# Score products over all 128 rows, and the memory's keys and values from split operands, in the second block of a two-block network

## The chip, the cores and the metric

The kernel runs on one core of a Trainium2 chip. The metric is the device time of one execution in microseconds (us), as the median of the runs. The core has five engines with a queue of their own each: TensorE (PE, with weight loads shown apart as PEld), VectorE (DVE), ScalarE (ACT), GpSimd (POOL) and SyncE (SP), which issues most of the transfers (DMA).

## The reference, cut to what matters

Two blocks of two layers each run over 512 tokens of width 1024. The change lies in the second block's token mixing: in the branch in which every query attends to selected keys (8 heads of 64), and in the branch that attends to a memory of 256 tokens (4 heads of 128).

```python
def dsa_branch(q, k, v, iq, ik, iw, positions):
    q = rotary(q.reshape(B, S, ATT_HEADS, ATT_HEAD_DIM), positions)
    k = rotary(k.reshape(B, S, ATT_HEADS, ATT_HEAD_DIM), positions)
    ...
    _, sel = lax.top_k(score, n_sel)                     # by the index heads
    s = jnp.einsum('bqhd,bqkhd->bqhk', qb, kg) * (ATT_HEAD_DIM ** -0.5)
    p = jax.nn.softmax(jnp.where(valid, s, -jnp.inf), axis=-1)
    return jnp.einsum('bqhk,bqkhd->bqhd', p, vg)

def memory_branch(mq, mem, w_mem_kv):
    kv = jnp.einsum('bmd,de->bme', mem, w_mem_kv)        # [256, 1024] @ [1024, 1024]
    mk, mv = jnp.split(kv, 2, axis=-1)
    s = jnp.einsum('bshd,bmhd->bhsm', q, mk) * (MEM_HEAD_DIM ** -0.5)
    return jnp.einsum('bhsm,bmhd->bshd', jax.nn.softmax(s, axis=-1), mv)
```

## The kernel before

Everything is computed in float32. A large product is made of three products of reduced operands: `split` (L368) writes a tensor as a high part (a cast on ACT, L370) and a low part (a subtraction on DVE, L371), and `mm3` (L361) multiplies high by high, high by low and low by high into one bank of PSUM. Weights come as units of 128 x 1024 (512 KB) through `Stream` (L1946): `next` loads a unit into one of 3 raw tiles and splits it into one of 4 pairs of the ring; `raw` (L1958) hands out the unit as it is. Large activations take one of 11 tiles of the pool `g8`.

`mixing_` (L1226) is one layer's token mixing in the second block. It first calls `memory_kv` (L1416), which makes the keys and values of the memory for the layer. There both operands are plain float32, not split: one float32 product is two passes on PE (two weight loads and two matmuls in the trace). `flush` then turns the last normalised tokens of the part before, and the projections follow: index keys and queries, then, merged, the index (which keys are selected), the memory's attention and other projections; then, merged again, `heads` (rotary queries and keys of two heads at a time), `attention` (L1504) and the gates.

For each pair of heads `heads` makes q of 2 planes and k of 3 planes of 512 tokens. A plane of q holds one head: its high part in 64 rows (partitions), its low part in the other 64. A plane of k holds that head's high part twice, in both halves, and the third plane the low parts of both heads, one in each half. A score tile is thus the product over 128 rows (high and low of q by high of k, L1515) plus a product over the 64 rows of q's high part and k's low part (L1516). There are 32 score tiles in a layer: 4 pairs of heads, 4 query tiles of 128 tokens and 2 heads, with 128, 256, 384 or 512 keys. The scores are followed by the softmax on DVE and ACT, the turn of the probabilities (L1528) and the product with the values (L1541).

The order of the instructions on each engine, and when a tile of a pool is taken, come from the framework's scheduler, which goes by priority in program order and by its own estimate of times; the kernel fixes the order only by how it merges the chains.

Of the kernel before, what the change touches and what calls it, by code (L numbers as in the profile page):

```python
# [11 lines left out]
F32 = mybir.dt.float32  # L12
# [24 lines left out]
# ---------------------------------------------------------------- host layout  # L37


def fm_unit(w, cols):  # L40
    """Columns `cols` of w [K, N] (-1: zeros) as a stationary unit [128, K/128 * len(cols)]."""
    k = w.shape[0] // 128
    cols = np.asarray(cols)
    out = np.zeros((128, k, len(cols)), w.dtype)
    on = cols >= 0
    out[:, :, on] = w.reshape(k, 128, -1)[:, :, cols[on]].transpose(1, 0, 2)
    return out.reshape(128, -1)


def tok_units(w, c, kp):  # L50
    """Rows of two k tiles and 512 columns of w as a moving unit [128, 2 * 512]."""
# [8 lines left out]
def cols(v):  # L60
    """[n * 128] -> [128, n]"""
# [7 lines left out]
def layout(i):  # L69
# [66 lines left out]
    # second block  # L136
# [58 lines left out]
def shape_constants():  # L195
# [14 lines left out]
    # frequency, phase (of a cosine), sign  # L210
# [19 lines left out]
# ---------------------------------------------------------------- the kernel  # L230


def merge(*chains):
    """Runs generators side by side; each (generator, share) yields what a step weighs, or None when it
    waits for another. The one that is furthest behind goes next."""
# [13 lines left out]
def pipeline(n, *stages):  # L249
    """Stage s of item i beside stage s + 1 of item i - 1."""  # L250
# [8 lines left out]
class Lane:  # L259
    """Tiles of one chain of work: its own slots, so that chains do not wait for each other's."""  # L260
# [27 lines left out]
class Net:  # L288
# [20 lines left out]
    def part(self, name):  # L309
        """Room on chip for a part of the work."""  # L310
# [6 lines left out]
    def phase(self, name):  # L317
        """The same with banks of PSUM."""
# [3 lines left out]
    # ---- small helpers  # L322
# [9 lines left out]
    def room(self, dt):  # L332
        """Small tiles in one of the raw ones, until it is full."""
# [15 lines left out]
    def new_h(self):  # L349
        """Token-major tiles [4][128, 1024]."""  # L350
# [3 lines left out]
    def row(self, L, name, n):  # L354
        """A row of DRAM on every partition."""
# [5 lines left out]
    def mm3(self, ps, a, b, start, stop):  # L361
        """ps (+)= a.T @ b for operands (high, low)."""
# [5 lines left out]
    def split(self, hi, lo, src, engine=None):  # L368
        """hi + lo = src, in parts that the PE carries exactly."""
# [3 lines left out]
    def rsqrt(self, L, v, n, scale=1.0, add=EPS):  # L373
        """(v * scale + add) ** -0.5 of [128, n] (more than 0)."""
# [26 lines left out]
    # ---- layer norm of token-major tiles into token-major h and feature-major (high, low)  # L401
# [10 lines left out]
    def ln_norm(self, L, t, gb, spill=None, light=()):  # L412
        """The layer norm of h[t], in place."""
# [3 lines left out]
    def ln_stats(self, L, src):  # L417
        """Of rows in two halves: what normalises them."""
# [11 lines left out]
    def ln_apply(self, L, t, gb, spill, stats, after=None, light=()):  # L430
        """The normalised rows into h[t]; `after`: what GpSimd does first; `light`: the tiles with both halves past
        the vector engine's longer forms."""
# [29 lines left out]
    def flush(self, L):  # L462
        """The turns that the part before has left, so that the PE does not wait for them."""
# [17 lines left out]
    # ---- products with the streamed weights  # L481
    def fm(self, L, u, x):
        """One tile of 128 output features, all tokens: PSUM [128, 512]."""
# [5 lines left out]
    def fm_first(self, lanes, us, x, L):  # L489
        """The first units of a part, one to a bank of each lane: the first half of the tokens, what is left of  # L490
        their turns, and the other half."""
# [11 lines left out]
    def tokmaj(self, L, st, x, use):  # L503
        """use(t, PSUM [128, 512]): token-major, one token tile after the other, over 8 k tiles."""
# [10 lines left out]
    def tokpart(self, L, st, lhs, kt, first):  # L515
        """h (token-major) += the product over kt k tiles, the tokens innermost."""
# [12 lines left out]
    def tokfinal(self, L, st, lhs, kt, first, done, turn=None):  # L529
        """As tokpart, one token tile after the other, each handed to done(t) and, two tiles later, to turn(t)."""  # L530
# [20 lines left out]
    # ---- statistics over features that lie on partitions  # L551
    def feat_r(self, L, sq, n):
        """(mean of the squares + eps) ** -0.5 of the tokens of each tile: [128, 4]."""
# [7 lines left out]
    def feat_rsqrt(self, L, sq, n):  # L561
        """Rows (mean of the squares + eps) ** -0.5 of all tokens on every partition: PSUM [128, 512]."""
# [1442 lines left out]
```

## Time and profile before

| | |
|---|---|
| median of 3 runs | 3082.91 us (3081.3 to 3084.93) |
| span of the profiled execution | 3080.9 us |
| PE, DVE, ACT, POOL busy | 96%, 70%, 46%, 15% of the span |
| memory stage of the first and the second layer | from about 1370 to 1402 us, from about 2214 to 2252 us |
| attention stage of the first and the second layer | from about 1572 to 1800 us, from about 2422 to 2650 us |

The profile is of one execution, whose first and last instruction lie 3080.9 us apart; the runs' median is 2.0 us above that. A line of an engine in the timeline gives start, duration, engine, line of the program, operation, the tile it writes and those it reads, the shape and how many were merged. Products on PE overlap: the cost of one is the distance to the next start, not its duration. "issue" stands for time in which an engine waited for nothing that the profile shows.

### The profile page before, as it was taken

Reading aid. Unit: us, or ns where it says so; the run is one execution under the profiler, and the core shown is the slowest. Engines: PE = TensorE matmul, PEld = TensorE weight load, DVE = VectorE, ACT = ScalarE, POOL = GpSimd, SP = SyncE. Lnnn points to the kernel's source line nnn. Section 1 sums busy time; section 2 is a strip of 40 time slices with the busy share of each in tenths; the row PEclk is TensorE's granted clock in tenths of the full one; section 3 lists DMA queues with packets and bytes.
Section 4 is the critical chain, followed back from the end, with each engine's and each line's share of the span. In section 5 each row is a group of like instructions: output and inputs, shape, how many; then the busy total and the mean of one; then the engine's idle time right before and its main releaser. Section 6 shows DMA issues by size and latency. Waiting matters only on the chain. (4 is left out here: it accounts for less than half of the span.)

```text
span 3080.9 us, 38491 instructions
## 1 busy us (share of the span) xinstructions
PE 2959.6 (96%) x14258; PEld 2306.5 (75%) x14258; DVE 2155.6 (70%) x3441; ACT 1432.6 (46%) x2230; POOL 463.6 (15%) x427
## 2 busy tenths in 40 slices
PE   7999999999999999999999997999899999979996
PEld 6777888888777888887777786777577777867774
DVE  6884756565976755666875447999758754479997
ACT  4443433334344433324534433888445344238884
POOL 4311100004211000011101103110311011031103
PEclk9999999998999999999999998999899999989998
DMA  5121233333120332335232256999441322569993
GB/s 185 50 74 42 84 96 96 99 115 104 49 76 28 104 97 97 101 130 158 59 94 75 82 205 222 366 385 384 163 143 57 93 78 83 198 221 358 384 382 123
DMA packets 128512, 457.25 MB, mean 148 GB/s; under 512 B 15744, under 2 KB 16832, under 8 KB 126912
## 3 DMA queue, kind: packets, MB, share of 16 engines
q1 hardware_dynamic: 117696, 425.37, 40.0%
q0 software_dynamic: 7168, 16.79, 1.7%
q10 hardware_dynamic: 3456, 12.58, 1.1%
q8 instruction: 114, 1.87, 0.2%
q14 instruction: 78, 0.64, 0.1%
HBM read 428.99 MB, written 27.26 MB: 148 GB/s over the span
## 5 line engine op out<-in xcount | busy, mean ns | idle before, releaser
L364 PE MATMUL AP<-g,hi 128*128 128x512 f32 (+1 forms) x1824 | 712.7, 391 | 6.1 <-DVE g L1321 2.6
L365 PE MATMUL AP<-g,hi 128*128 128x512 f32 (+1 forms) x1824 | 703.0, 386 | 3.7 <-DVE g L371 3.7
L366 PE MATMUL AP<-g,lo 128*128 128x512 f32 (+1 forms) x1824 | 703.9, 386 | 0.0
L371 DVE TENSOR_TENSOR lo<-raw,hi 128x1024 fp32r<-128x1024 f32 x306 | 393.5, 1287 | 373.2 <-ACT hi L370 364.1
L370 ACT CAST hi<-raw 128x1024 fp32r<-128x1024 f32 x318 | 333.5, 1050 | 607.0 <-PE AP L365 406.7
L364 PEld LDWEIGHTS AP<-g,hi 128*128 128x128 f32 x1824 | 346.9, 190 | 81.8 <-issue 8.2
L365 PEld LDWEIGHTS AP<-g,hi 128*128 128x128 f32 x1824 | 347.2, 190 | 71.5 <-issue 4.3
L366 PEld LDWEIGHTS AP<-g,lo 128*128 128x128 f32 x1824 | 346.9, 190 | 68.8 <-issue 2.6
L371 DVE TENSOR_TENSOR lo<-g,hi 128x1024 fp32r<-128x1024 f32 x204 | 239.1, 1218 | 23.7 <-ACT hi L370 23.2
L370 ACT CAST hi<-g 128x1024 fp32r<-128x1024 f32 x204 | 207.0, 1050 | 50.5 <-PE AP L366 32.7
L371 DVE TENSOR_TENSOR lo<-wide,hi 128x1024 fp32r<-128x1024 f32 x180 | 211.0, 1217 | 23.9 <-ACT hi L370 23.4
L365 PE MATMUL HP<-lo,Txt 128*96 128x512 f32 x512 | 203.7, 398 | 0.0
L366 PE MATMUL HP<-hi,Txt 128*96 128x512 f32 x512 | 203.5, 397 | 0.0
L364 PE MATMUL HP<-hi,Txt 128*96 128x512 f32 x512 | 201.5, 400 | 1.1 <-ACT Txt L370 1.1
L370 ACT CAST hi<-wide 128x1024 fp32r<-128x1024 f32 x180 | 182.7, 1050 | 22.3 <-PE HP L366 18.3
L364 PE MATMUL AP<-hi,g 128*128 128x512 f32 x384 | 159.6, 419 | 2.7 <-DVE g L880 2.7
L366 PE MATMUL AP<-hi,g 128*128 128x512 f32 x384 | 152.9, 400 | 0.0
L365 PE MATMUL AP<-lo,g 128*128 128x512 f32 x384 | 152.3, 398 | 0.0
L364 PE MATMUL BP<-hi,g 128*128 128x512 f32 x352 | 136.8, 390 | 0.0
L365 PE MATMUL BP<-lo,g 128*128 128x512 f32 x352 | 136.6, 389 | 0.0
L366 PE MATMUL BP<-hi,g 128*128 128x512 f32 x352 | 134.0, 389 | 0.0
L1203 POOL TENSOR_TENSOR Bw<-Bw,Bw 128x512 f32<-128x512 f32 x26 | 43.7, 1681 | 459.0 <-DVE Bw L1202 384.0
(497 smaller groups left out, 5235.3 us busy)
## 6 DMA issues: line engine op xcount, KB each, us to landing
wide<-in_wmoeu SPq DMA_DIRECT2D x64, 1024.0 KB, 8.5
g<-in_wmoeu SPq DMA_DIRECT2D x64, 1024.0 KB, 8.1
raw<-in_wup SPq DMA_DIRECT2D x88, 512.0 KB, 3.5
g<-in_wmoed SPq DMA_DIRECT2D x34, 1024.0 KB, 8.6
wide<-in_wmoed SPq DMA_DIRECT2D x30, 1024.0 KB, 8.2
raw<-in_xwin SPq DMA_DIRECT2D x50, 512.0 KB, 3.7
raw<-in_xgate SPq DMA_DIRECT2D x48, 512.0 KB, 3.6
raw<-in_wdown SPq DMA_DIRECT2D x44, 512.0 KB, 3.5
```

The costliest lines, as they stand in the source:

```text
L364: mm(ps, a[0], b[0], start=start, stop=False)
L365: mm(ps, a[0], b[1], start=False, stop=False)
L366: mm(ps, a[1], b[0], start=False, stop=stop)
L370: self.nc.scalar.copy(hi, src)
L371: (engine or self.nc.vector).tensor_tensor(out=lo, in0=src, in1=hi.bitcast(F32), op=OP.subtract)
L1203: nc.gpsimd.tensor_tensor(out=u, in0=u, in1=sw, op=OP.add)
```

## The change

Three edits, all in the second block. k gets a fourth plane, so that the low part of each head has a plane of its own, with zeros in the other 64 rows (written by POOL); the second score product then runs over 128 rows, like the first. `memory_kv` splits the memory (4 pieces of two k tiles) and its weights into high and low and uses `mm3` in place of the float32 products; the two parts of the memory take two more tiles of `g8` while it runs. The pool weights `pw` and the value bias `bv` are allocated and loaded in the part `xmem`, after the index queries, in place of the start of `mixing_`. Comments and docstrings are removed too.

```diff
@@ mixing_
-        pw = kept("pw")
-        nc.sync.dma_start(pw, self.A[f"poolw{l}"])
-        bv = kept("bv")
-        src = self.A[f"bv{l}"]
-        nc.sync.dma_start(bv, bass.AP(tensor=src.tensor, offset=src.offset, ap=[[0, 128], [1, 512]]))
...
         with self.part(f"xmem{l}"):
+            pw, bv = kept("pw"), kept("bv")
+            nc.sync.dma_start(pw, self.A[f"poolw{l}"])
+            src = self.A[f"bv{l}"]
+            nc.sync.dma_start(bv, bass.AP(tensor=src.tensor, offset=src.offset, ap=[[0, 128], [1, 512]]))
...
-                q, k = (self.pp.tile([128, n, S], FR, tag="qk%d" % n, bufs=1, name=self.nm("qk")) for n in (2, 3))
+                q, k = (self.pp.tile([128, n, S], FR, tag="qk%d" % n, bufs=1, name=self.nm("qk")) for n in (2, 4))
...
                     ac.copy(k[at, i], rot[at])
-                    ve.tensor_tensor(out=k[at, 2], in0=rot[at], in1=k[at, i].bitcast(F32), op=OP.subtract)
+                    ve.tensor_tensor(out=k[at, 2 + i], in0=rot[at], in1=k[at, i].bitcast(F32), op=OP.subtract)
+                    nc.gpsimd.memset(k[to, 2 + i].bitcast(F32), 0.0)
                     ac.copy(k[to, i], rot[at])
@@ memory_kv
+        mem = [self.g8(FR, (128, 8, 256)) for _ in range(2)]
+        for i in range(4):
+            c = slice(2 * i, 2 * i + 2)
+            self.split(mem[0][:, c], mem[1][:, c], raw[:, c])
...
-            u = ms.raw()
+            u = ms.next()
             ps = L.P((128, 256))
             for k in range(8):
-                mm(ps, u[:, k * 128:(k + 1) * 128], mem[:, k], start=k == 0, stop=k == 7)
+                self.mm3(ps, tuple(a[:, k * 128:(k + 1) * 128] for a in u), tuple(a[:, k] for a in mem), k == 0, k == 7)
...
-            u = ms.raw()
+            u = ms.next()
...
-                    mm(vp[t], mem[:, k, t * 128:t * 128 + 128], u[:, j * 512:(j + 1) * 512], start=k == 0, stop=k == 7)
+                    self.mm3(vp[t], tuple(a[:, k, t * 128:t * 128 + 128] for a in mem),
+                             tuple(a[:, j * 512:(j + 1) * 512] for a in u), k == 0, k == 7)
@@ attention, scores
-            r = slice(64 * hh, 64 * hh + 64)
             n = 128 * (t + 1)
             ps = L.P((128, n))
-            nc.tensor.matmul(ps, q[:, hh, t * 128:n], k[:, hh, :n], start=True, stop=False)
-            nc.tensor.matmul(ps, q[r, hh, t * 128:n], k[r, 2, :n], start=False, stop=True)
+            for p in (hh, 2 + hh):
+                nc.tensor.matmul(ps, q[:, hh, t * 128:n], k[:, p, :n], start=p == hh, stop=p != hh)
```

## Rows read from the trace of the kernel before

**Rows 1.** The page: span, and busy time of each engine.
```profile
span 3080.9 us, 38491 instructions
PE 2959.6 (96%) x14258; PEld 2306.5 (75%) x14258; DVE 2155.6 (70%) x3441; ACT 1432.6 (46%) x2230; POOL 463.6 (15%) x427
```
**Rows 2.** Stages: length, PE, PEld, DVE, ACT, POOL busy, clock, DMA share, GB/s.
```profile
1370.00:1402.00 32.00, 30.29 (x121) 20.43 (x119) 23.31 (x57) 10.22 (x17) 5.17 (x6) 1.00 0.57 176
1572.00:1800.00 228.00, 227.21 (x1070) 171.11 (x1069) 122.08 (x260) 96.15 (x178) 19.70 (x14) 1.00 0.27 81
2201.00:2222.00 21.00, 15.03 (x46) 9.24 (x45) 19.88 (x31) 4.45 (x6) 17.66 (x17) 0.87 0.77 293
2222.00:2252.00 30.00, 29.86 (x112) 19.61 (x110) 8.72 (x13) 7.93 (x14) 1.48 (x2) 0.92 0.44 152
```
**Rows 3.** Timeline of PE's products: a score pair with 256 keys and what follows.
```profile
1585.48 0.28 PE L1515 MATMUL IP<-qk,qk 128*128 128x256 f32 x1
1585.69 0.38 PE L1516 MATMUL IP<-qk,qk 64*128 64x256 f32 x1
1586.00 0.50 PE L366 MATMUL AP<-g,lo 128*128 128x512 f32 x1
1586.33 0.40 PE L364 MATMUL AP<-g,hi 128*128 128x512 f32 x1
```
**Rows 4.** Timeline of PE's weight loads at the same pair.
```profile
1585.68 0.18 PEld L1516 LDWEIGHTS IP<-qk,qk 64*128 64x128 f32 x1 [0.24 <-issue]
1585.99 0.19 PEld L366 LDWEIGHTS AP<-g,lo 128*128 128x128 f32 x1
1586.10 0.19 PEld L364 LDWEIGHTS AP<-g,hi 128*128 128x128 f32 x1
```
**Rows 5.** Timeline of PE's products: a score pair with 512 keys.
```profile
1594.54 0.40 PE L1515 MATMUL IP<-qk,qk 128*128 128x512 f32 x1
...
1595.29 0.50 PE L366 MATMUL AP<-g,lo 128*128 128x512 f32 x1
```
**Rows 6.** Timeline of PE's products: index score pairs, 256 and 512 columns.
```profile
1437.07 0.40 PE L1397 MATMUL IP<-ik,g 128*128 128x256 f32 x2
1437.30 0.39 PE L366 MATMUL AP<-g,lo 128*128 128x512 f32 x1
1437.54 0.40 PE L364 MATMUL AP<-g,hi 128*128 128x512 f32 x1
...
1521.47 0.63 PE L1397 MATMUL IP<-ik,g 128*128 128x512 f32 x2
1521.93 0.39 PE L365 MATMUL AP<-lo,g 128*128 128x512 f32 x1
```
**Rows 7.** The tiles of q and k: the second score product, its forms and number.
```profile
L1516 PE MATMUL IP<-qk,qk x64: 322/411/502, 1574.1 to 2593.9; 64*128 64x128 f32 x16, 64*128 64x256 f32 x16, 64*128 64x384 f32 x16, 64*128 64x512 f32 x16
```
**Rows 8.** Groups by line on POOL: count, busy us, mean ns, idle before.
```profile
L1778 POOL MEMSET g<- 96x2048 f32 x4 | 7.2, 1810 | 140.8 <-PE AP L366 135.7 <-DVE Bw L1327 5.1
```
**Rows 9.** Timeline of PE: the memory's keys and values, first layer.
```profile
1370.79 7.07 PE L1427 MATMUL AP<-g,raw 128*128 128x256 f32 x32
...
1389.95 12.28 PE L1435 MATMUL AP<-raw,g 128*128 128x512 f32 x28 [1.72 <-DMA raw<-in_wmem]
```
**Rows 10.** Timeline of PE: split products of 256 columns, first block.
```profile
709.46 0.28 PE L366 MATMUL GP<-g,lo 128*128 128x256 f32 x1
709.58 0.28 PE L364 MATMUL GP<-g,hi 128*128 128x256 f32 x1
```
**Rows 11.** Groups by line and form: the subtractions of a split.
```profile
L371 DVE TENSOR_TENSOR lo<-raw,hi 128x1024 fp32r<-128x1024 f32 x11 | 13.5, 1223 | 6.3 <-ACT hi L370 6.2
L371 DVE TENSOR_TENSOR g<-IP,g 128x512 fp32r<-128x512 f32 x4 | 2.8, 688 | 1.3 <-ACT g L370 1.3
```
**Rows 12.** Timeline of PE: the memory's second head, second layer.
```profile
2221.42 6.28 PE L1427 MATMUL AP<-g,raw 128*128 128x256 f32 x16 [3.83 <-ACT wide L440]
```
**Rows 13.** The stage view around it, columns as in rows 2.
```profile
2220.00:2226.00 6.00, 4.58 (x11) 3.68 (x12) 3.73 (x6) 1.15 (x2) 3.38 (x4) 0.50 0.81 302
```

More of the change, by code (lines that the diff above doesn't have):

```diff
@@ L1414, in index, with memory_kv @@
             ve.tensor_scalar(sc, sc, -3e38, NEG, op0=OP.not_equal, op1=OP.mult)
-    def memory_kv(self, L, l, mem):
+    def memory_kv(self, L, l, raw):
         nc = self.nc
@@ L1419, in memory_kv @@
         ms = self.stream(f"wmem{l}")
+        mem = [self.g8(FR, (128, 8, 256)) for _ in range(2)]
+        for i in range(4):
+            c = slice(2 * i, 2 * i + 2)
+            self.split(mem[0][:, c], mem[1][:, c], raw[:, c])
         kv = self.g8()
         mk = kv[:, 0:2].rearrange("p a (b c) -> p (a b) c", b=2)
-        mm = nc.tensor.matmul
         for h in range(4):
-            u = ms.raw()
+            u = ms.next()
             ps = L.P((128, 256))
             for k in range(8):
-                mm(ps, u[:, k * 128:(k + 1) * 128], mem[:, k], start=k == 0, stop=k == 7)
+                self.mm3(ps, tuple(a[:, k * 128:(k + 1) * 128] for a in u), tuple(a[:, k] for a in mem), k == 0, k == 7)
             ac.copy(mk[:, h], ps)
```

## The prediction

> **What bounds the kernel now.** I read the page first: TensorE (PE) is busy 2959.6 of 3080.9 us, 96%, VectorE (DVE) 70%, ScalarE 46% [rows 1]. A busy PE need not be a PE at its peak, so the second view is the table by stage. In the attention stage of a layer (1572 to 1800) PE is busy 227.21 of 228 us while DVE has 122.08: PE sets the pace there, and what is saved on PE is saved in time. In the memory stage of the first layer (1370 to 1402) PE has 30.29 of 32, but DVE already has 23.31; before that of the second layer (2201 to 2222) DVE has 19.88 of 21 and PE 15.03, so there the layer norm on DVE is the bound, and in 2222 to 2252 it is PE again with 29.86 of 30 [rows 2]. The third view is the order of PE's instructions, where not the printed durations count (products are pipelined: 0.39 us each, 0.24 apart [rows 6]) but the distance from one start to the next.
>
> **Part 1, score products over 128 rows.** A score tile is two products: L1515 over 128 rows, L1516 over 64. With 256 keys L1515 starts at 1585.48, L1516 at 1585.69, the next projection product at 1586.00, the one after it at 1586.33: the pair takes 0.52 us, and the product behind it 0.33 [rows 3]. Why: the weight load of L1516 (64 rows) starts at 1585.68, when the product before it has left, instead of beside it, and the load for the 128-row product behind it starts only at 1585.99, again with nothing left to hide it [rows 4]. With 512 keys the pair takes 1594.54 to 1595.29, 0.75 us [rows 5]. The nearest row to what replaces it is the index score of the same kernel: two products over 128 rows, one stationary tile for both. With 256 columns the pair takes 1437.07 to 1437.30, 0.23 us, and the product behind it 0.24; with 512 columns 1521.47 to 1521.93, 0.46 us [rows 6]. So a pair of 256 gives back 0.52 + 0.33 - 0.23 - 0.24 = 0.38 us, a pair of 512 gives 0.75 - 0.46 = 0.29 plus the same 0.1 behind it, 0.39. For 384 keys I take 0.38 too; for 128 keys both products are short and the weight loads themselves become the limit, an estimate of 0.25. There are 64 pairs in the two layers [rows 7], 16 of each width: 16 x (0.25 + 0.38 + 0.38 + 0.39) = 22.4 us. The 0.1 behind a pair is lost only where a wide product follows; without it for any pair the sum is 16 us. I take **20 us**, nearer the upper end since projection products fill the stage, as in rows 3, and keep 15 to 23.
>
> What else the part adds: a fourth plane of k and 16 memsets of 64 x 512 on GpSimd (POOL). The nearest row, a memset of 96 x 2048, takes 1.81 us [rows 8], so an estimate of 0.45 each; POOL has 19.70 busy us of the 228 in this stage [rows 2], and a memset needs nothing but the free plane. It is queued ahead of the rotary and gate additions on POOL; if it waited for the plane until the last scores of the heads before, those additions would wait too, but k's other planes wait for the same release now. Cost 0, up to 1 us per pair of heads if that cover failed (8 us in all). The subtractions and copies stay the same in number and size.
>
> A rule speaks against this part. The Trainium skill, "TensorE: Matmul & The Clock Gate", Part 3, says that a weight load overlaps running products only when its row group differs. By that rule a load over all rows could never run beside a product over all rows, part 1 would give nothing and the sum would be 3081 us, as in rival (b). The trace differs: a load over 128 rows (L364) starts at 1586.10 beside a product over 128 rows that began at 1586.00 and lasts 0.50, and it is the change of rows that is paid [rows 3, 4, 6].
>
> **Part 2, memory keys and values from split operands.** Now 64 key products (32 in the code, two passes each) run 0.216 us apart: (7.07 - 0.38) / 31, the last one's own duration of about 0.38 taken off; the 32 value passes likewise (12.28 - 0.59) / 27 = 0.43 us apart [rows 9]. Per layer 64 x 0.216 + 32 x 0.43 = 27.6 us of PE. After: 96 key products and 48 value products at one pass. The 256-column one costs 0.12 us [rows 10], the 512-column one 0.23 [rows 6]: 11.5 + 11.0 = 22.5 us. PE gains 5 us per layer if it is fed.
>
> Feeding it is new work: eight weight units per layer, each a cast on ScalarE (10.22 us busy of 32 in this stage, so not the bound [rows 2]) and a subtraction of 1.22 us on DVE, and the memory itself, four casts and four subtractions of 0.69 us [rows 11]: 8 x 1.22 + 4 x 0.69 = 12.5 us of DVE, where before the raw tiles went straight to PE. First layer: DVE would have 23.31 + 12.5 = 35.8 us in a stage of 32. If all of it had to end first, the stage grows by 4; but the sine and cosine tables that are made on DVE in the same stretch are needed only behind the first projection, and can give way. The start is the other cost: PE now goes straight from the feed-forward products into the keys at 1370.79; after the change it needs at least one memory piece and one unit from DVE (0.69 + 1.22 = 1.9 us, at most 4.0 with all four pieces), and their buffers come free only as the feed-forward products end. So -5 + 3 = **-2 us** in this layer, between -7 (the weights' landing wait of 1.72 us goes too [rows 9]) and +4. Second layer: PE starts its second head at 2221.42 because a bank waits for the layer norm [rows 12]; DVE before it has 1.1 us free of 21 [rows 2]. Either the subtractions go in between and the norm ends 2 to 4 us later, or they come behind it and PE starts as much later; the 5 us pay for that. **0 us**, between -4 and +5. Earlier release of raw tiles lets the weight loads start sooner; I count nothing for it.
>
> **Part 3, the pool weights and the value bias** are loaded later by SyncE's queue. Two short issues per layer move behind the first projections' loads; their users (the value projection and the pooling) come after other projections. 0 us, by estimate 1 later at most.
>
> **Sum**: 3080.9 - 20 - 2 = 3058.9 us of span; the median of the runs lies 2.0 above the span (3082.91), so **3061 us**.
>
> **The rivals.** (a) *DVE becomes the bound of the memory stages.* The 12.5 us go in full onto a full engine: +4 in the first layer, +5 in the second instead of -2. For it: 19.88 of 21. Against it: 8.72 of 30 just behind it [rows 2]. Time 3082.9 - 20 + 9 = 3072. (b) *The full-row pair stalls as the mixed one does*, so the change doesn't do what it says: scores give 0, memory -2 to +9, 3081 to 3092, as likely as not within the bound of no change. Against it: rows 6 is the same form of product. (c) *Slower through the clock.* In 2220 to 2226, after an idle stretch of PE, the granted clock is 0.50, 1.2 of 2.4 GHz, and products take twice as long [rows 13]. If in both memory stages PE got its units so late that it stayed at that level throughout, 22.5 us of products would take 45 in each layer: +45 - 10 against today, and 3082.9 - 20 + 35 = 3098. It decides from the point where DVE delivers a unit more slowly than every 5.6 us (twice 22.5 / 8); a unit costs DVE 1.22, so four others would have to go ahead of each. A single fall of the clock for 6 us costs 3 and lies in the range. (d) *Better fed*: no start delay and no cold stretch, -7 and -4 with 22 from the scores: 3050.
>
> **How the numbers follow.** Forecast (3061, give or take the terms' bounds) 0.66, (a) 0.16, (d) 0.08, (b) 0.05, (c) 0.05. A measurement of this kernel tells about 0.2%, 6 us, from no change. Forecast, (a) and (d) are faster by more than that, but the lower ends of the scores (15) and of the memory stages (+9) together reach the bound: faster 0.87, within it 0.08, slower 0.05. Range: from (d) to just past (a), 3050 to 3074.
>
> **What would show it.** Right: no weight load of 64 rows; pairs of 256 near 0.24 us and the product behind them near 0.23; the attention stage shorter by about 10 us in each layer with PE still full; key products 0.12 apart. Wrong: pairs that still take 0.5 us; a PE that waits for the low parts in the memory stage by more than 5 us; the clock at 0.50 there for longer than now; POOL's additions behind the memsets late and PE idle in the attention stage; or a gain in attention that the stages behind it give back.

## The result, and the profile after

The changed kernel takes **3064.65 us** (median of 4 runs, 3062.45 to 3067.21) against 3082.11 of the kernel before, run beside it: a ratio of 0.9948, 95% interval 0.9936 to 0.9961. That is 17.5 us faster, 3.7 us slower than the forecast of 3061, and inside the range. The profiled execution has a span of 3062.8 us, 18.0 less than the one before.

Where the 18 us lie is read from landmarks in the two traces: starts of the same instructions, and how far apart they are. The stretches are: up to the last feed-forward product of the first block; the **memory stage** of a layer, from that product (second layer: from the first of the products that add the last expert's rows) to the first index score; the **index stage** up to the first attention score; the **attention stage** up to the last product with the values. Change against before, in us:

| stretch | predicted | after |
|---|---|---|
| up to the first memory stage (code untouched) | 0 | -2.5 |
| memory stage, first layer | -2 | +1.9 |
| index stage, first layer | 0 | -1.1 |
| attention stage, first layer | -10 | -10.7 |
| memory stage, second layer | 0 | +5.7 |
| index stage, second layer | 0 | -0.6 |
| attention stage, second layer | -10 | -10.7 |
| all the rest | 0 | 0.0 |
| span | -22 | -18.0 |

In the untouched stretch the executions shown below differ by -6.6 to +1.4 us from the one before, whatever was changed behind it. So from here on stages are compared, and spans only where whole runs are.

The page of the kernel after, its span and busy times, answers [rows 1]:

```profile
span 3062.8 us, 38785 instructions
PE 2926.7 (96%) x14354; PEld 2310.4 (75%) x14354; DVE 2184.2 (71%) x3465; ACT 1451.7 (47%) x2254; POOL 473.6 (15%) x443
```

The table by stage answers [rows 2] (length, busy time of PE, PEld, DVE, ACT, POOL, granted clock, DMA share, GB/s):

```profile
1370.00:1402.00 32.00, 26.98 (x161) 24.44 (x162) 29.99 (x58) 15.90 (x23) 5.80 (x5) 0.89 0.61 186
1560.00:1788.00 228.00, 227.21 (x1117) 179.46 (x1116) 132.09 (x278) 100.45 (x185) 24.88 (x21) 1.00 0.28 87
2188.00:2213.00 25.00, 14.62 (x54) 9.32 (x52) 24.93 (x34) 9.82 (x13) 17.92 (x15) 0.88 0.72 268
```

PE lost 33 us of busy time and the span 18: the rest, 15 us, is new idle time of PE. In the attention stage PE is full as before (227.21 of 228), so there what it no longer does is gained in full. In the memory stages the picture has turned round: DVE is now the full engine, 29.99 of 32 in the first layer and 24.93 of 25 in the second, and PE is the one that waits.

The score pairs in PE's timeline (start, duration, engine, line, operation, tiles, shape, number merged), 256 keys and then 512, answer [rows 3, 5]:

```profile
1582.47 0.39 PE L365 MATMUL AP<-g,hi 128*128 128x512 f32 x1
1582.69 0.40 PE L1519 MATMUL IP<-qk,qk 128*128 128x256 f32 x2
1582.93 0.39 PE L366 MATMUL AP<-g,lo 128*128 128x512 f32 x1
1583.16 0.39 PE L364 MATMUL AP<-g,hi 128*128 128x512 f32 x1
...
2434.48 0.62 PE L1519 MATMUL IP<-qk,qk 128*128 128x512 f32 x2
2434.94 0.40 PE L366 MATMUL AP<-g,lo 128*128 128x512 f32 x1
```

The two weight loads of the first pair answer [rows 4]:

```profile
1582.47 0.41 PEld L1519 LDWEIGHTS IP<-qk,qk 128*128 128x128 f32 x2
```

The pair of 256 takes 1582.69 to 1582.93, 0.24 us where it took 0.52, and the product behind it 0.23 where it took 0.33; the pair of 512 takes 0.46 where it took 0.75. Its loads start at 1582.47, beside the running product L365. All 128 score products have 128 rows now, where the second one had 64 [rows 7]; from the tile's group:

```profile
L1519 PE MATMUL IP<-qk,qk x128: 218/333/505, 1571.3 to 2575.7; 128*128 128x128 f32 x32, 128*128 128x256 f32 x32, 128*128 128x384 f32 x32, 128*128 128x512 f32 x32
```

The zeros take 0.53 us a memset on GpSimd, where 0.45 was estimated from [rows 8]; from its groups by line:

```profile
L1302 POOL MEMSET qk<- 64x512 f32 x16 | 8.5, 534 | 26.2 <-PE IP L1519 25.7
```

The memory products in PE's timeline (in brackets the wait in front and what ended it), the first layer and then the second, down to the window projection, answer [rows 9, 10, 12]:

```profile
1368.22 0.36 PE L364 MATMUL AP<-g,hi 128*128 128x256 f32 x1
1373.05 0.58 PE L365 MATMUL AP<-g,hi 128*128 128x256 f32 x1 [4.46 <-DVE g L371]
1373.43 0.41 PE L366 MATMUL AP<-g,lo 128*128 128x256 f32 x1
1373.64 0.41 PE L364 MATMUL AP<-g,hi 128*128 128x256 f32 x1
...
1383.47 0.39 PE L364 MATMUL AP<-g,hi 128*128 128x256 f32 x1 [1.72 <-ACT g L1431]
1383.70 0.28 PE L365 MATMUL AP<-g,hi 128*128 128x256 f32 x1
1383.82 0.28 PE L366 MATMUL AP<-g,lo 128*128 128x256 f32 x1
...
2207.99 0.28 PE L366 MATMUL AP<-g,lo 128*128 128x256 f32 x1
2216.34 0.58 PE L364 MATMUL AP<-g,hi 128*128 128x256 f32 x1 [8.07 <-ACT wide L440]
...
2243.03 0.73 PE L364 MATMUL AP<-g,hi 128*128 128x512 f32 x2 [1.95 <-ACT g L370]
```

First layer: the first product goes at 1368.22, the second waits 4.46 us for the memory's low part (L371 on DVE), and the granted clock is then 0.50 (1.2 of 2.4 GHz) until 1377.3, in which a product costs 0.21 us; later, at 1.00, it costs 0.12. Second layer: the first head is done at 2208, and the second waits 8.07 us for its bank, which the last activation of the layer norm (L440 on ScalarE) has to read first. Before, that wait was 3.83 us [rows 12]. At the end the window projection waits 1.95 us for a cast of the activations on ScalarE. What the norm waited for stands in DVE's timeline:

```profile
2194.25 2.24 DVE L371 TENSOR_TENSOR lo<-raw,hi 128x1024 fp32r<-128x1024 f32 x1
...
2197.01 0.69 DVE L422 BATCH_NORM_STATS2 Hs<-TP 128x6 f32<-128x512 f32 x1
...
2198.22 1.20 DVE L371 TENSOR_TENSOR lo<-raw,hi 128x1024 fp32r<-128x1024 f32 x1
2199.35 0.68 DVE L441 TENSOR_TENSOR wide<-wide,g 128x512 f32<-128x512 f32 x1
...
2201.89 3.33 DVE L371 TENSOR_TENSOR g<-g,g 128x512 fp32r<-128x512 f32 x2
2205.14 0.20 DVE L424 BATCH_NORM_AGGREGATE Hs<-Hs 128x2 f32<-128x12 f32 x1
2205.26 1.23 DVE L371 TENSOR_TENSOR g<-g,g 128x512 fp32r<-128x512 f32 x2
```

L422, L424 and L441 are the norm, L371 the new subtractions: the scheduler has put them between the norm's steps. With two more at 2208.34 and 2212.36 (1.21 us each), 10.4 us of subtractions stand inside the second layer's norm. In the first layer it is the same on a smaller scale; two of its rows:

```profile
1368.19 2.35 DVE L371 TENSOR_TENSOR lo<-raw,hi 128x1024 fp32r<-128x1024 f32 x2
...
1372.31 1.89 DVE L371 TENSOR_TENSOR g<-g,g 128x512 fp32r<-128x512 f32 x3
```

With one more of the first form ahead of these (1365.78), one of the second at 1374.72 and one of the first at 1377.11, 7.3 us of new subtractions stand ahead of the first layer's last L441.

So a memory stage is best read in three pieces: **norm** (from the stage's start to the start of the last L440), **products** (from there to the first product of the window projection that follows), **behind** (from there to the first index score). Before they take 6.9, 25.4 and 27.9 us in the first layer and 20.0, 32.0 and 27.8 us in the second. Change against before, for this kernel and those of the experiments:

| kernel | first layer: norm, products, behind | second layer: norm, products, behind |
|---|---|---|
| after | +7.3, -5.3, -0.1 | +7.6, -4.5, +2.7 |
| scores_only | 0.0, -0.8, -0.1 | 0.0, 0.0, +0.1 |
| memory_only | +7.3, -5.3, 0.0 | +7.7, -4.4, +2.5 |
| norm_first | +7.3, -4.8, 0.0 | +0.5, +2.7, +2.4 |
| norm_first_but_one | +7.2, -5.3, -0.1 | +4.2, -1.0, +2.6 |
| split_first_layer | +7.3, -5.3, -0.1 | +0.8, -0.2, 0.0 |
| splits_beside | +7.2, +0.3, -0.1 | +7.4, -0.2, +1.1 |
| values_split | 0.0, 0.0, -0.1 | +0.6, -0.3, +3.7 |
| high_only | -0.1, +1.5, +4.8 | +0.6, -2.2, +0.3 |
| high_flush | 0.0, -2.9, 0.0 | -0.4, -4.8, +2.5 |

### The profile page after: what moved, and what is told of

Its sections match the earlier page's. It is cut to its first block, busy times and chain, and to the rows that moved or that the text cites. A ratio compares the mean times of both kernels' runs of the same rounds, so it can differ in the third digit from the quotient of the medians.

```text
span 3062.8 us, 38785 instructions
## 1 busy us (share of the span) xinstructions
PE 2926.7 (96%) x14354; PEld 2310.4 (75%) x14354; DVE 2184.2 (71%) x3465; ACT 1451.7 (47%) x2254; POOL 473.6 (15%) x443
## 5 line engine op out<-in xcount | busy, mean ns | idle before, releaser
L364 PE MATMUL AP<-g,hi 128*128 128x512 f32 (+1 forms) x1888 | 730.5, 388 | 16.6 <-ACT wide L440 8.1
L365 PE MATMUL AP<-g,hi 128*128 128x512 f32 (+1 forms) x1888 | 722.2, 383 | 10.7 <-DVE g L371 10.7
L366 PE MATMUL AP<-g,lo 128*128 128x512 f32 (+1 forms) x1888 | 722.1, 383 | 0.0
L371 DVE TENSOR_TENSOR lo<-raw,hi 128x1024 fp32r<-128x1024 f32 x322 | 413.3, 1285 | 370.2 <-ACT hi L370 361.1
L370 ACT CAST hi<-raw 128x1024 fp32r<-128x1024 f32 x334 | 350.0, 1051 | 614.8 <-PE AP L365 406.2
L364 PEld LDWEIGHTS AP<-g,hi 128*128 128x128 f32 x1888 | 360.8, 191 | 88.4 <-ACT wide L440 8.3
L365 PEld LDWEIGHTS AP<-g,hi 128*128 128x128 f32 x1888 | 361.4, 191 | 78.9 <-DVE g L371 12.5
L366 PEld LDWEIGHTS AP<-g,lo 128*128 128x128 f32 x1888 | 361.1, 191 | 67.1 <-issue 1.9
L371 DVE TENSOR_TENSOR lo<-g,hi 128x1024 fp32r<-128x1024 f32 x204 | 239.1, 1218 | 23.8 <-ACT hi L370 23.3
L371 DVE TENSOR_TENSOR lo<-wide,hi 128x1024 fp32r<-128x1024 f32 x180 | 211.1, 1217 | 23.0 <-ACT hi L370 22.6
L365 PE MATMUL HP<-lo,Txt 128*96 128x512 f32 x512 | 203.5, 397 | 0.0
L364 PE MATMUL AP<-hi,g 128*128 128x512 f32 x416 | 172.9, 419 | 2.7 <-DVE g L880 2.7
L366 PE MATMUL AP<-hi,g 128*128 128x512 f32 x416 | 165.2, 399 | 0.0
L365 PE MATMUL AP<-lo,g 128*128 128x512 f32 x416 | 165.0, 397 | 0.0
L365 PE MATMUL BP<-lo,g 128*128 128x512 f32 x352 | 136.6, 389 | 0.0
L379 POOL TENSOR_TENSOR Bs<-Bs,mhalf 128x1 f32<-128x1 f32 x8 | 7.8, 980 | 685.9 <-DVE Bs L378 685.9
```

The lines of the kernel that those rows point to most:

```text
L364: mm(ps, a[0], b[0], start=start, stop=False)
L365: mm(ps, a[0], b[1], start=False, stop=False)
L366: mm(ps, a[1], b[0], start=False, stop=stop)
L370: self.nc.scalar.copy(hi, src)
L371: (engine or self.nc.vector).tensor_tensor(out=lo, in0=src, in1=hi.bitcast(F32), op=OP.subtract)
L379: self.nc.gpsimd.tensor_tensor(out=r, in0=x, in1=self.mhalf[:, 0:n], op=OP.pow)
```

## The experiments

The theory after the result: the score products gave what they promised, and the memory's split costs time because its subtractions stand in the norm's chain. Times below are medians; the ratio is to the kernel before, run beside each group of kernels.

**1. Each part alone.** Four kernels: full-row scores with the memory's products as before; the split memory with the scores as before; only the moved loads; and full-row scores without the zeros (this one adds the product of a query's low part with the other head's low part).

```diff
# scores_only: memory_kv of the kernel before
-            u = ms.next()
+            u = ms.raw()
...
-                self.mm3(ps, tuple(a[:, k * 128:(k + 1) * 128] for a in u), tuple(a[:, k] for a in mem), k == 0, k == 7)
+                mm(ps, u[:, k * 128:(k + 1) * 128], mem[:, k], start=k == 0, stop=k == 7)
# memory_only: scores of the kernel before
+            r = slice(64 * hh, 64 * hh + 64)
...
-            for p in (hh, 2 + hh):
-                nc.tensor.matmul(ps, q[:, hh, t * 128:n], k[:, p, :n], start=p == hh, stop=p != hh)
+            nc.tensor.matmul(ps, q[:, hh, t * 128:n], k[:, hh, :n], start=True, stop=False)
+            nc.tensor.matmul(ps, q[r, hh, t * 128:n], k[r, 2, :n], start=False, stop=True)
# move_only: both of these
# no_zeros: scores_only with three planes, no memset, and
-            for p in (hh, 2 + hh):
+            for p in (hh, 2):
```

> The changed kernel with the memory's keys and values made as before (float32 products, no splits); the full-row scores and the later loads of pool weights and bias stay. Theory (the score products alone bring the gain, the splits take some of it back): the two attention stages are 10.6 us shorter each, as in the changed kernel, and the memory stages are as before, so 3082 - 21 = 3061 us, 4 us faster than the changed kernel. Rival (the splits are worth something and the 5 us lost ahead of the second layer's projections have another cause, such as the later loads): 3066 to 3068, slower than the changed kernel.

> The changed kernel with the score products as before (second one over 64 rows, k of 3 planes, no zeros); the split operands of the memory and the later loads stay. Theory: slower than the kernel before by what the trace shows lost in the second layer less what the first gives, 5.4 - 0.5 - about 1: 3085 to 3087 us. Rival (PE's 5 us per layer come through): 3072 to 3078.

> The kernel before with the loads of pool weights and value bias moved alone. Theory: nothing waits for them, 3082 within 1.5 us. Rival (they are the cause of the 1.2 us gained between the first layer's memory stage and its attention, or of part of the loss in the second layer): more than 2 us to either side.

> As the first of these, but k has 3 planes again, there are no memsets, and the second product runs over all 128 rows of the shared low plane (it adds a product of two low parts to the scores). Theory (what was paid is the change of row count, and memsets and fourth plane cost nothing): the same time as with the zeros, 3061 within 1.5 us. Rival (the 16 memsets hold up GpSimd's additions): 2 to 8 us faster than with the zeros.

Measured: scores_only 3057.38 us, ratio 0.9923 (0.9909 to 0.9936); memory_only 3085.1 us, 1.0013 (1.0004 to 1.0023); move_only 3079.73 us, 0.9995 (0.9986 to 1.0004); no_zeros 3057.24 us, 0.9923 (0.991 to 0.9937). In scores_only both attention stages are 10.7 us shorter, as in the full change, and both memory stages stand as before (-0.9 and 0.0). In memory_only the attention stages change by 0.0, and the memory stages by +1.9 and +5.8. So the two parts add up, the whole gain is the scores', and the memory's split is a loss of some 7 us: **scores_only beats both kernels**. The zeros and the fourth plane cost nothing (10.7 and 10.8 us gained without them). The moved loads alone come out 2.9 us below the kernel before, on the rival's side, but the interval includes no change. Their trace shows -1.0 us in the first memory stage and -1.1 in the first index stage, nearly the same in scores_only (-0.9 and -1.0), and which waits shrink: PE's wait for a weight unit of the memory goes from 1.72 us [rows 9] to 0.79,

```profile
1387.76 0.70 PE L1434 MATMUL AP<-raw,g 128*128 128x512 f32 x1 [0.79 <-DMA raw<-in_wmem]
```

and a wait of 0.93 us early in the index stage, for a subtraction on DVE (L1211), is gone.

**2. What a pair of mixed row counts costs.** One head of two keeps the 64-row product.

```diff
-            for p in (hh, 2 + hh):
-                nc.tensor.matmul(ps, q[:, hh, t * 128:n], k[:, p, :n], start=p == hh, stop=p != hh)
+            r = slice(0, 128) if hh else slice(0, 64)
+            nc.tensor.matmul(ps, q[:, hh, t * 128:n], k[:, hh, :n], start=True, stop=False)
+            nc.tensor.matmul(ps, q[r, hh, t * 128:n], k[r, 2 + hh, :n], start=False, stop=True)
```

> The kernel with full-row score products and whole operands for the memory, but the second product of a pair runs over 64 rows again for the even head of each pair of heads, and over 128 rows for the odd one; nothing of the result changes. If the cost is one of each pair that mixes 64 and 128 rows, half of the pairs pay it: the two attention stages lose about half of their 21 us again, some 3068 us (3066 to 3070), and the 256-key pairs of one trace have two durations, near 0.23 and near 0.52 us. Rival (the cost is paid only where the rows change from pair to pair, or where the 64 rows are the upper ones): 3057 or 3078 us.

Measured: 3067.66 us, ratio 0.9962 (0.9948 to 0.9975); each attention stage 5.2 us shorter than before, against 10.7 with all pairs full. PE's timeline has both kinds side by side in one execution:

```profile
2414.73 0.50 PE L1515 MATMUL IP<-qk,qk 128*128 128x128 f32 x2
2415.16 0.38 PE L1516 MATMUL IP<-qk,qk 64*128 64x256 f32 x1
2415.47 0.50 PE L365 MATMUL AP<-g,hi 128*128 128x512 f32 x1
2415.81 0.22 PE L1516 MATMUL IP<-qk,qk 128*128 128x128 f32 x1
...
2425.46 0.28 PE L1515 MATMUL IP<-qk,qk 128*128 128x256 f32 x1
2425.58 0.28 PE L1516 MATMUL IP<-qk,qk 128*128 128x256 f32 x1
2425.69 0.39 PE L366 MATMUL AP<-g,lo 128*128 128x512 f32 x1
2425.93 0.39 PE L364 MATMUL AP<-g,hi 128*128 128x512 f32 x1
```

The 64-row product holds PE for 0.31 us (2415.16 to 2415.47), the 128-row one for 0.11 (2425.58 to 2425.69), with the same 256 columns; the product behind the mixed pair takes 0.34, behind the full one 0.24. The cost is one of each pair that mixes 64 and 128 rows: when half the pairs are mixed, half of the gain is left. The rivals, a price paid once per run of pairs or only for the upper half of the rows, fall. That a 64-row product is dear by itself is another rival. Against it stands a place in the kernel before where two 64-row products, of opposite halves of the rows and of 128 and 256 columns, follow each other (the first row has both):

```profile
1628.22 0.39 PE L1516 MATMUL IP<-qk,qk 64*128 64x128 f32 x2
1628.54 0.50 PE L364 MATMUL AP<-g,hi 128*128 128x512 f32 x1
```

Both together hold PE for 0.32 us, no longer than the single one of 256 columns between 128-row products (0.31 [rows 3]). Two of the same half were not tried.

**3. Is it the order on DVE?** If the subtractions hurt because they stand ahead of norm steps, issuing them behind the norm should help. Second layer only; in norm_first all of them, in norm_first_but_one all but the memory's own and the first unit's.

```diff
# norm_first; self.normed is the last instruction L441 of a norm
-            self.split(mem[0][:, c], mem[1][:, c], raw[:, c])
+            with self.tc.issue_after(self.normed.ins) if l else nullcontext():
+                self.split(mem[0][:, c], mem[1][:, c], raw[:, c])
...
-            u = ms.next()
+            with self.tc.issue_after(self.normed.ins) if l else nullcontext():
+                u = ms.next()
# norm_first_but_one: the second edit alone, for the key units with `if l and h`
```

> The changed kernel, with one difference: in the second layer all splits of the memory's keys and values (the low part of the memory and of every weight unit on VectorE) are issued behind the last multiplication of the layer norm on VectorE, so that they no longer stand inside the norm's chain. Theory (the second layer lost its 5.7 us because splits stood ahead of norm work on a full VectorE, which opened the lane's bank late): the norm ends some 7 us earlier, at the place it has without the split, but the splits (about 21 us of VectorE for this stage, of which less than half fits behind the norm) now come behind it and TensorE waits for them instead; from the moe's end to the first index product the loss goes from 5.7 to between 0 and 3 us, so 3059 to 3062 us. Rival (the loss is simply that VectorE has some 15 us more to do in a stage that it bounds, wherever they stand): 5 us or more are lost as before, 3064 us or above.

> As the kernel before it, but the low part of the memory and the first weight unit's split keep the place that they have in the changed kernel; only the later units' splits of the second layer stand behind the norm. Theory of the order: the first head's products run beside the norm (in the changed kernel they did so), only some 4.5 us of subtractions stay inside the norm's chain, the loss of the second layer's memory stage is 0 to 3 us, 3058 to 3062 us. Rival (the sum of VectorE's work decides, not its order): 3064 us.

Measured: 3066.62 us, ratio 0.9953 (0.994 to 0.9967), and 3066.07 us, 0.9947 (0.9933 to 0.996). Both expectations of the theory fall: the second memory stage is +5.7 and +5.8 us, as with the scheduler's own order. The pieces show why. In norm_first the norm is back in its place (+0.5 instead of +7.6), but what it gained the products lost (+2.7 instead of -4.5), as DVE's timeline in norm_first shows:

```profile
2212.82 0.68 DVE L441 TENSOR_TENSOR wide<-wide,g 128x512 f32<-128x512 f32 x1
2213.42 3.56 DVE L371 TENSOR_TENSOR g<-g,g 128x512 fp32r<-128x512 f32 x4
2216.90 3.48 DVE L371 TENSOR_TENSOR lo<-raw,hi 128x1024 fp32r<-128x1024 f32 x3
```

and PE's:

```profile
2211.99 0.58 PE L364 MATMUL AP<-g,hi 128*128 128x256 f32 x1 [7.41 <-ACT wide L440]
...
2218.17 0.39 PE L366 MATMUL AP<-g,lo 128*128 128x256 f32 x1 [2.61 <-DVE lo L371]
```

PE has no memory product complete before the norm's end, where the kernel before had a whole head done, and it starts at 2218 behind the subtractions. DVE is full either way (24.71 us of the 25 from 2195 to 2220 in norm_first), so in the three orders tried the order decides only which wait is seen.

**4. One layer alone.**

```diff
-        kv = self.memory_kv(A, l, raw)
+        kv = (self.memory_kv_plain if l else self.memory_kv)(A, l, raw)
```

> The changed kernel with the memory's keys and values of the second layer from whole operands as before, and of the first layer from split ones. If the layers' costs simply add: the time of the kernel with full-row score products alone (3057.4 us) and 2 to 3 us for the first layer, 3059 to 3060.5 us; the second layer's memory stage then stands as in the kernel before (no loss). Rival (the first layer's splits give back what they cost, since the shorter TensorE work is 5 us): 3055 to 3057 us; rival (the two layers' costs are one and the same wait, moved): 3063 us or more.

Measured: 3061.03 us, ratio 0.9933 (0.9919 to 0.9946): first memory stage +1.9 us, as with both layers split, and the second +0.7 in place of +5.7. The layers' costs are separate and add (the time is 0.5 us above the range stated for that, and well below the rival's 3063).

**5. DVE's work against PE's waiting.** Two kernels that take the split apart. high_only leaves out the subtractions: each triple of products runs over the high parts three times. splits_beside keeps every split, and PE runs the old whole products over the high parts. In both the memory's keys and values carry rounded operands.

```diff
# high_only
-            self.split(mem[0][:, c], mem[1][:, c], raw[:, c])
+            ac.copy(mem[0][:, c], raw[:, c])
+        mem[1] = mem[0]
...
-            u = ms.next()
+            u = ms.high()        # a raw unit and its cast, as (hi, hi)
# splits_beside
-                self.mm3(ps, tuple(a[:, k * 128:(k + 1) * 128] for a in u), tuple(a[:, k] for a in mem), k == 0, k == 7)
+                mm(ps, u[0].bitcast(F32)[:, k * 128:(k + 1) * 128], mem[0].bitcast(F32)[:, k], start=k == 0, stop=k == 7)
... (the value products likewise)
```

> The changed kernel without the subtractions that make the low parts of the memory and of its weights, in both layers: the high parts (the copies on ScalarE) stay, and each triple of products runs over the high parts three times, so that the memory's keys and values carry rounded operands. TensorE has the same products as in the changed kernel and VectorE about 12 to 13 us less per memory stage. Theory (VectorE's added subtractions are what cost both stages, wherever they stand): the second layer's 5.7 us of loss between the moe's end and the first index product turns into a gain of 2 to 5 us, and the first layer's 2 us into a gain of 2 to 5, so 3047 to 3053 us. Rival (the shorter TensorE work meets a bank, a unit's load or a low clock that would have come anyway): no loss but no gain, 3056 to 3058 us. Rival (the subtractions are not the cause): 3063 to 3065 us.

> The changed kernel with all splits of the memory and its weights as they are, but the products as before, one whole product in place of three, over the high parts (the memory's keys and values so carry rounded operands); no product waits for a low part any more. Theory (the added VectorE and ScalarE work costs the norm's chain and the stage behind it by itself): TensorE has its 27.6 us again and the norm's chain still ends some 7 us late, so the second layer loses 5 to 10 us and the first 0 to 3 us, 3063 to 3070 us. Rival (TensorE's waiting for the low parts was the whole cost): near the kernel with full-row scores alone, 3056 to 3059 us.

Measured: high_only 3062.3 us, ratio 0.994 (0.9927 to 0.9953); splits_beside 3076.74 us, 0.9989 (0.998 to 0.9997). In splits_beside no product waits for a low part and PE has its old products (pieces +0.3 and -0.2), yet the norm ends 7.2 and 7.4 us late and the memory stages are 7.4 and 8.3 us longer, more than expected. PE now waits for the norm itself: in the first layer for one of its additions on GpSimd (L443) and then 2.65 us for a bank, in the second 10.43 us for L440.

```profile
1382.12 0.33 PE L459 MATMUL IP<-c_ident,g 128*128 128x128 f32 x1 [3.68 <-POOL g L443]
```

In high_only, which has the changed kernel's casts and products but no subtractions, the norm is in place (-0.1 and +0.6). Together: the subtractions alone delay the norm by 7 us in either layer, and where no shorter products pay for it, the stage grows by the whole delay. But high_only did not gain what the theory said. Its second memory stage is 1.3 us shorter; its first is 6.3 longer. ScalarE's timeline in high_only shows the first layer:

```profile
1397.59 0.63 ACT L604 ACTIVATE sin<-Lw 128x512 f32<-128x512 f32 x1 [1.90 <-DVE Lw L603]
...
1399.08 1.04 ACT L370 CAST hi<-raw 128x1024 fp32r<-128x1024 f32 x1 [0.39 <-DMA raw<-in_xwin]
1400.04 1.55 ACT L370 CAST g<-IP 128x512 fp32r<-128x512 f32 x3
```

and PE's:

```profile
1395.59 1.14 PE L459 MATMUL IP<-c_ident,g 128*128 128x128 f32 x9
1401.64 1.22 PE L364 MATMUL AP<-g,hi 128*128 128x512 f32 x2 [4.91 <-ACT g L370]
```

PE ran out of memory products at 1395.59, did the transposes of the normalised activations only then, and waited 4.91 us for their casts (g<-IP), which stood in ScalarE's queue behind a sine table and a weight unit that were themselves waiting. Behind that wait the granted clock was 0.50 (1398.8 to 1409.0), and that is most of the 4.8 us lost behind the products. The scheduler had put the transposes behind the products; that it did so because it no longer saw a busy DVE is a guess.

**6. The same with that order mended.** high_only with the transposes ahead of the value products.

```diff
+        self.flush(I)                      # in memory_kv, ahead of the value products
         vp = [L.P() for _ in range(2)]
```

> The kernel high_only (no subtractions for the memory's and its weights' low parts, products three times over the high parts, so the memory's keys and values carry rounded operands) with one step moved: the transposes of the normalised activations are issued ahead of the value products in place of behind them. In high_only the first layer lost 6 us although the norm ended as early as in the kernel before, since TensorE ran out of memory products 5 us early and then waited 5.2 us for the split of those transposes, which ScalarE made only at 1400 us. Theory (the shorter memory products pay once VectorE's norm is left alone and the activations are ready): the first layer's 6 us of loss becomes a gain of 2 to 6 us, the second layer stays at its gain of 1 to 2 us, 3050 to 3054 us. Rival (something else is due no earlier, the window weights or the rotation tables): the wait stays at the same place under another name, 3058 to 3063 us.

Measured: 3051.82 us, ratio 0.9913 (0.9896 to 0.9929); memory stages -3.0 and -2.7 us. The theory holds: without the subtractions, and with the activations ready, the shorter products pay, and this is the most they paid here: of 5.1 us less PE work a layer about 3 arrive. In the second layer 4.8 are gained at the products and 2.5 given back behind them, where PE waits another 0.64 us and the granted clock is 0.50 from 2229.8 to 2233.2.

**7. A split that DVE could afford.** The keys from whole operands, the values alone split, in the second layer behind the norm.

```diff
-            u = ms.next()
+            u = ms.raw()
...
+                mm(ps, u[:, k * 128:(k + 1) * 128], raw[:, k], start=k == 0, stop=k == 7)
...
+        with self.tc.issue_after(self.normed.ins) if l else nullcontext():
+            for i in range(4):
+                c = slice(2 * i, 2 * i + 2)
+                self.split(mem[0][:, c], mem[1][:, c], raw[:, c])
... (the value units likewise behind the norm)
```

> Full-row score products; the memory's keys from whole operands as before, its values alone from split ones (the memory's split and that of the four value units; in the second layer these are issued behind the last multiplication of the norm on VectorE). The four value units take 32 half-speed passes near 0.43 us before (13.7 us) and 48 products near 0.227 us after (10.9 us), so 2.9 us less TensorE work per layer, and the subtractions for them, about 5 us for the units and 6 us for the memory, have the key products' 14 us to run beside, behind the norm. Theory (VectorE's work hurts only where it stands beside the norm): 2 to 3 us are gained per layer against full-row scores alone, 3051 to 3055 us. Rival (whatever is split there is paid for in the stage): 3057 to 3061 us.

Measured: 3060.4 us, ratio 0.9938 (0.9925 to 0.9952): the rival's time, and by the medians 3 us, by the ratios 4.6 us slower than scores_only. The norm is in place in both layers (0.0 and +0.6), and still nothing is gained at the products, and 3.7 us are lost behind them in the second layer. Again ScalarE's timeline tells why:

```profile
2233.89 1.05 ACT L370 CAST hi<-raw 128x1024 fp32r<-128x1024 f32 x1 [2.62 <-DMA raw<-in_xwin]
2234.85 1.06 ACT L1444 COPY g<-AP 128x512 f32<-128x512 f32 x2
...
2236.75 1.57 ACT L370 CAST g<-IP 128x512 fp32r<-128x512 f32 x3
```

The casts of the activations, for which the window projection waits, come at 2236.75, behind a weight unit whose load landed late (2.62 us of waiting) and the values' copies. PE idled 3.4 us before that projection, which takes what the products had gained, and its granted clock in 2237 to 2247 was 0.66, which is where most of the 3.7 us behind them went. In the first layer, too, the granted clock fell among the value products, to 0.50 from 1388.4 to 1391.8, behind a wait of 1.92 us for a cast.

## Why the prediction was right, and where it was wrong

**The scores: right in size and reason.** -20 forecast, -21.4 measured in the traces (10.7 a layer), within 15 to 23. The pair of 256 came out at 0.24 as read from [rows 6], the product behind it at 0.23. For 128 keys 0.25 was estimated and 0.24 measured for the pair itself (0.41 before, 0.17 after). The rule of the Trainium skill that was weighed there ("TensorE: Matmul & The Clock Gate", Part 3, in its list of what overlaps: weight loads overlap only with products of another row group) would have left the span at 3081. The trace disagrees: the 128-row loads at 1582.47 run beside the 128-row product of 1582.47, and experiment 2 shows that what is paid is the change of rows. The zeros cost nothing, as said; no_zeros shows it.

**The first memory stage: -2 forecast, +1.9 measured, inside -7 to +4.** The term that was mis-sized is the start. It was put at 1.9 to 4.0 us for the first piece and unit; the wait was 4.46, and it was followed by two things that the term did not have: 21 products at a clock of 0.50, which cost 0.09 us more each (2.0 us), and 1.72 us for a bank whose eviction stood on ScalarE behind the late norm. The step that failed with it is that "the sine and cosine tables ... can give way". They did: they start 21.7 us into the stage where they started at 14.3. But before the change they stood behind the norm, whose last L441 came at 7.8, and so the room that they left was no use to subtractions that PE needs at the stage's start. There DVE had little room already (in the kernel before it is busy 7.52 us of the 8 from 1362 to 1370 and 5.94 of the 7.3 from 1369.7 to 1377), and the norm gave way too, by 7.3 us, as much as the subtractions ahead of its end take (7.3). The 5.1 us gained by the products and the 1.72 us of waiting for a weight unit that went away [rows 9], less 4.46 + 2.0 + 1.72 and a last wait of 0.25, leave a loss of 1.6; the stage lost 1.9.

**The second memory stage: 0 forecast, +5.7 measured, just outside -4 to +5.** The step "either the subtractions go in between and the norm ends 2 to 4 us later, or they come behind it and PE starts as much later; the 5 us pay for that" had both ways right (the changed kernel is the first, norm_first the second) and the size wrong. 10.4 us of subtractions stood inside the norm and it ended 7.6 us late; the products then paid back 4.5, as said; and 2.7 more were lost behind them, which no term had: after the wait of 1.95 us for ScalarE's cast the window projection waited 0.43 us more for a subtraction, and its granted clock was 0.66 in 2243 to 2248, with 8 products 0.43 us apart in place of 0.23 (1.6 us).

**Rival (a) was the better account of the memory.** It had +4 and +5 for the memory stages. The trace shows +1.9 and +5.7, 7.6 of its 9, where the forecast had -2. That the time came out nearer to the forecast (3061) than to (a) (3072) is owed to the 1.4 us more that the scores gave, to 1.4 less lost in the memory stages, to 1.7 gained in the index stages, which neither account had, and to 2.5 of variation ahead of the change, which is luck. The stated evidence against (a), DVE's 8.72 of 30 us behind the norm, did not decide: PE's products stand ahead of that room, or are pushed into it. Rival (b) fell with the first pair. Rival (c) happened in stretches of a few us (0.50 from 1370.6 to 1377.3, from 2203.5 to 2206.9, from 2216.3 to 2220.3 and from 2244.4 to 2247.9), not throughout. So one of the signs of being wrong did show, a clock at 0.50 for longer than before (1.00 in the first memory stage [rows 2]), and another, a wait of more than 5 us for the low parts, was missed by little (4.46). Rival (d) had the memory stages at -7 and -4; high_flush, without the subtractions, reached -3.0 and -2.7.

**The moved loads: 0 forecast, about -1.0 in the first memory and -1.1 in the first index stage** in move_only, below what the runs can tell. The -1.0 is the weight unit's shorter wait (experiment 1); in the changed kernel PE has no wait for these units left, so there it is not counted. The index stage's gain is in every kernel with the moved loads, between 0.8 and 1.2 but for no_zeros (0.3).

What stays open: whether another engine could make the low parts without touching the norm. Making them on GpSimd was not run; in the kernel after, its subtractions of 128x1024 take 2.57 us each elsewhere in the trace, and the norm uses GpSimd too. Open also is why the second index stage is 0.6 us shorter.

## What to carry to other kernels

A cheaper product is a gain only in a stage that its engine bounds: before trading PE time for DVE work, read DVE's row of the very stretch, and which chain on DVE the next stage waits for; here 7 us of added subtractions made that chain 7 us later, and putting them elsewhere only moved the wait. Room on an engine counts only if it lies ahead of the step that needs it. A product that was long enough to cover a norm is work and cover at once, and when it gets shorter the casts and loads of the stage behind it must come earlier too. Mixed row counts in one accumulation, on the other hand, were worth padding with zeros in a stage that PE fills (227.21 us of 228): 21.4 us over 64 pairs, 0.33 us each.

## What the runs showed of the hardware that was not expected

Two subtractions of 128x512 took 3.33 us together from 2201.89, beside two additions of the norm on GpSimd (2.95 us from 2201.71), and the next two, beside none, 1.23 us. One of 128x1024 took 2.24 us from 2194.25, beside GpSimd's additions up to 2195.4, and 1.20 us from 2198.22, beside nothing on GpSimd. The Trainium skill ("SBUF — State Buffer", "SBUF: two separate sides") says that VectorE, with two inputs from SBUF, and GpSimd hold one pair of ports in turn, each for a whole instruction. The trace agrees with that here; no run was made to separate it. So a part of the 7.6 us by which the norm was late in the second layer may be this and not the subtractions' own time: an estimate from these rows is 3.1 of their 10.4 us (2.24 - 1.20 and 3.33 - 1.23). In the first layer the subtractions ahead of the norm's end took their usual 1.2 and 0.69 us, and it was late all the same.
